# A decoder step on one Trainium2 core: cached keys and values laid out with 16 rows of one sample on each partition

## The chip, the cores and the metric

The kernel runs on one core of a Trainium2 chip. The metric is the device time of one execution in microseconds (us). A core has a matmul engine (PE, with its weight loads listed as PEld), a vector engine (DVE), an activation engine (ACT), a general engine (POOL) and a queue engine that issues most transfers (SP). Each engine works through its own queue in the order in which the program was built, and its head waits until what it needs has been signalled.

## The reference, cut to what matters

One step of a two-layer decoder is computed for a prompt group (256 positions of one sequence) and a sample group (8 samples, one position each) that share the weights. All data is fp32. Each layer has two SwiGLU blocks, a mixer and a cross attention. The change concerns the cross attention of the 8 samples, whose keys and values come from a cache in memory (256 rows, 4 heads, 256 numbers per head, for each sample and layer: 8 MB of keys and 8 MB of values per layer).

```python
def cross_attn(x, mk, mv, w_q, w_o):
    B, T, D = x.shape
    q = (x @ w_q).reshape(B, T, X_HEADS, X_HEAD_DIM)
    s = jnp.einsum('bthd,bnhd->bhtn', q, mk.astype(q.dtype)).astype(jnp.float32) / math.sqrt(X_HEAD_DIM)
    p = jax.nn.softmax(s, axis=-1).astype(x.dtype)
    o = jnp.einsum('bhtn,bnhd->bthd', p, mv.astype(x.dtype)).reshape(B, T, D)
    return o @ w_o
...
    y_sample, conv_s, rec_s = trunk(x_sample, state_conv, state_rec, cache_mem_k, cache_mem_v)
```

## The kernel before, in words

Activations lie transposed: the model dimension on the 128 partitions, the 256 prompt positions and 8 samples side by side as 264 columns. Every large product is made of three matmuls (each factor is split into a high and a low part; low times low is left out), lines 300 to 302 for the projections and 826 to 828 for the prompt's keys and values (tile `kv`). The weights come in pieces of 512 KB into the tiles `raw` (line 94, issued by SP); ACT rounds each to `wh` (line 105), and DVE or POOL subtracts to make `wl` (line 117). In the four `kv` blocks of an attention stage the subtraction is on POOL, since `W.lo` is set to `("p",)` there.

`attention(l, norm, nxt)` runs once per layer. It projects the queries of four heads (`project`, tile `qT` per head), makes the prompt's keys and values head by head (`do_kv`, 48 matmuls each, in 8 pieces of 6), and then the output projection. Smaller work is written as Python generators in three lanes; between pieces of large matmuls `flow.tick()` lets each lane emit its next piece up to the next `yield`. So a lane's piece lands on every engine's queue between two pieces of the large product. Lane 0 holds the samples: `sample_scores(h)` for four heads, then `sample_rest`. Lane 1 holds the prompt's attention: `transpose_k` (PE tile `pkt`, DVE copy to `KTt`), `prompt_scores` (PE `psc`, softmax with DVE `mxp` and ACT and DVE `Pp`, PE transposes `ppt`, then ACT `PTh` and DVE `PTl`) and `prompt_values` (PE `po`, ACT `oh`, DVE `ol`). `Vh` and `Vl` (lines 843 and 844) are the split values of the prompt. A scheduler that builds the program may move pieces within each engine's queue by data and by its own priorities; what it made is read from the built order.

The samples, before. Keys come through a ring of four 1 MB tiles (`Ring`, four free slots; a slot is refilled when `ring.done` is called). A key tile of `fill_k(h, hf)` holds one head of four samples; partition p holds rows p and 128 + p of each of them. `sample_scores(h)`:

- ACT copies the 8 query columns of head h to `zq`, rounded; DVE subtracts to put the rest 32 columns further (line 868).
- Two PE transposes (`pz`, line 872) and an ACT copy make `qn`: the queries as rows.
- For each sample a PE matmul with a picked column as weights (`pick`, line 880, tile `pb`) puts this sample's query of 256 numbers on all 128 partitions. They are issued in pairs: 4 pairs per head, 16 per layer, 32 in the program.
- For each sample and each half of its rows DVE multiplies a key row with the query and adds up (line 885, `tensor_tensor_reduce`, tile `junk`; a second short instruction writes the sum to `sc`): 16 per head, 64 per layer.

`sample_rest`: PE turns `sc` (`pst`, line 962, 2 transposes), a softmax over 32 rows of 256 follows on DVE and ACT (lines 903 to 911), PE turns it back (`psp`, line 968), DVE spreads it (line 970) into `PTs`, where the other samples' columns are zero. Then for each sample b and each half of its rows, four matmuls (one per head, line 979, tile `spv`) with a value tile of sample b (`fill_v(b)`, line 639). Each value tile gives its ring slot back after its 8 matmuls.

Of the kernel before, what the change touches and what calls it, by code (L numbers as in the profile page):

```python
# [16 lines left out]
P = 128  # L17
# [10 lines left out]
RH = 8  # L28
EPS = 1e-6
# [187 lines left out]
def trunk_step(ctx: ExitStack, tc: tile.TileContext, ins, consts, outs, stop=None):  # L217
# [22 lines left out]
    sel = cp.tile([P, NB], F32R, name="sel")  # L240
    fs, ks, vs = (cp.tile([P, RH, NB], F32, name=n) for n in ("fs", "ks", "vs"))
# [280 lines left out]
    def prepare():  # L522
# [64 lines left out]
        nc.vector.tensor_add(sel, ident[:, :NB], ident[:, 32 : 32 + NB])  # L587
        mt = ring.tiles["masks"]
# [37 lines left out]
    def add_cache(l):  # L626
        def fill_k(h, hf):
            def f(t):
                rows = ins["cache_mem_k"][l, 4 * hf : 4 * hf + 4].rearrange("b n h d -> (b n) h d")
                nc.sync.dma_start(  # L630
                    t.rearrange("p (c d) -> p c d", d=XD), rows[:, h].rearrange("(c p) d -> p c d", p=P)
                )

            return f

        def fill_v(b):
            def f(t):
                rows = ins["cache_mem_v"][l, b].rearrange("(t p) h d -> p t (h d)", p=P)
                nc.sync.dma_start(t.rearrange("p (t e) -> p t e", t=2), rows)
# [6 lines left out]
        for b in range(NB):  # L646
            ring.add((l, "v", b), fill_v(b))
# [137 lines left out]
    def attention(l, norm, nxt):  # L785
        with tc.tile_pool(name="at", bufs=1) as ap:
# [5 lines left out]
            sc = ap.tile([P, 2, XH * NB], F32, name="sc")  # L792
            PTs = ap.tile([P, 2, XH, 9 * NB], F32, name="PTs")
            os = ap.tile([P, XD], F32, name="os")
            nc.gpsimd.memset(PTs, 0.0)
            nc.gpsimd.memset(os, 0.0)
            zq = ap.tile([P, 2, P], F32, name="zq")
            nc.gpsimd.memset(zq, 0.0)
# [64 lines left out]

            def sample_scores(h):
                qT, z = qTs[h], zq
                zr = z.bitcast(F32R)
                nc.scalar.copy(zr[:, :, :NB], qT[:, :, T:])
                nc.vector.tensor_sub(z[:, :, 32:40], qT[:, :, T:], z[:, :, :NB])
                yield
                pz = aux_bank("pz")  # L870
                for dt in range(2):
                    nc.tensor.transpose(pz[:, dt * P : dt * P + P], z[:, dt], ident)
                qn = ap.tile([P, XD], F32R, tag="qn", name="qn", bufs=2)
                nc.scalar.copy(qn, pz[:, :XD])
                yield
                for b2 in range(NB // 2):
                    pb = aux_bank("pb")
                    t = ring.tiles[l, "k", h, b2 // 2].rearrange("p (b t d) -> p b t d", b=4, t=2)
                    for i in range(2):
                        nc.tensor.matmul(pb[:, i * XD : i * XD + XD], pick(2 * b2 + i), qn, start=True, stop=True)  # L880
                    for i in range(2):
                        b = 2 * b2 + i
                        for nt in range(2):
                            junk = ap.tile([P, XD], F32, tag="junk", name="junk", bufs=1)
                            nc.vector.tensor_tensor_reduce(  # L885
                                junk,
                                t[:, b % 4, nt],
                                pb[:, i * XD : i * XD + XD],
                                1.0,
                                0.0,  # L890
                                ALU.mult,
                                ALU.add,
                                sc[:, nt, h * NB + b : h * NB + b + 1],
# [596 lines left out]
```

## Time and profile before

| what | value |
|---|---|
| median of 3 runs (lowest, highest) | 1320.15 us (1319.61, 1321.84) |
| time of the profiled execution | 1320.33 us |
| its span in the trace | 1318.5 us |
| granted TensorE clock, mean | 0.996 |
| attention of layer 0, of layer 1 (about) | 300 to 395 us, 1000 to 1110 us |

Times in the trace are in us from the start of the span. A busy share of PE counts a matmul from its start to its modelled end, and matmuls overlap, so what one costs in a stream is read from the distance between starts. In a row of the timeline stand the start, the duration, engine, line, operation, output and inputs with their shapes, and in brackets the idle time just before and what ended it. In a row of windows stand the stretch, its length, then for PE, PEld, DVE, ACT and POOL the busy us and the count, then the granted clock, the share of the DMA engines and GB/s.

### The profile page before, as it was taken

Reading aid. Unit: us, or ns where it says so; the run is one execution under the profiler, and the core shown is the slowest. Engines: PE = TensorE matmul, PEld = TensorE weight load, DVE = VectorE, ACT = ScalarE, POOL = GpSimd, SP = SyncE. Lnnn points to the kernel's source line nnn. Section 1 sums busy time; section 2 is a strip of 40 time slices with the busy share of each in tenths; the row PEclk is TensorE's granted clock in tenths of the full one; section 3 lists DMA queues with packets and bytes.
Section 4 is the critical chain, followed back from the end, with each engine's and each line's share of the span. In section 5 each row is a group of like instructions: output and inputs, shape, how many; then the busy total and the mean of one; then the engine's idle time right before and its main releaser. Section 6 shows DMA issues by size and latency. Waiting matters only on the chain. (4 is left out here: it accounts for less than half of the span.)

```text
span 1318.5 us, 26128 instructions
## 1 busy us (share of the span) xinstructions
PE 1295.1 (98%) x10392; PEld 1251.1 (95%) x10392; DVE 827.2 (63%) x1570; ACT 688.2 (52%) x1121; POOL 294.1 (22%) x240
## 2 busy tenths in 40 slices
PE   8999999999999999999999999999999999999997
PEld 7999999999868999999999999999999788999996
DVE  6555567759825655556555445978699637766454
ACT  6454444455445545544555544655664446666442
POOL 3211331221732111132111231000023531211220
PEclk9999999999999999999999999999999999999998
DMA  8796555646997666656666556555457994776650
GB/s 280 224 301 180 167 183 177 192 153 204 347 362 210 195 178 178 182 169 192 188 180 178 179 176 188 161 171 162 133 159 242 386 331 131 238 208 208 193 175 34
DMA packets 265147, 266.75 MB, mean 202 GB/s; under 512 B 8697, under 2 KB 259577, under 8 KB 265026
## 3 DMA queue, kind: packets, MB, share of 16 engines
q1 hardware_dynamic: 259198, 259.78, 63.6%
q10 hardware_dynamic: 5828, 5.32, 1.2%
q8 instruction: 81, 1.33, 0.4%
q14 instruction: 40, 0.33, 0.1%
HBM read 255.00 MB, written 10.07 MB: 201 GB/s over the span
## 5 line engine op out<-in xcount | busy, mean ns | idle before, releaser
L117 DVE TENSOR_TENSOR wl<-raw,wh 128x1024 fp32r<-128x1024 f32 (+1 forms) x347 | 425.2, 1230 | 247.1 <-ACT wh L105 232.5
L300 PE MATMUL pj<-xh,wh 128*128 128x264 f32 x1952 | 560.6, 287 | 2.0 <-DVE xT L717 2.0
L301 PE MATMUL pj<-xl,wh 128*128 128x264 f32 x1952 | 553.5, 284 | 0.0
L302 PE MATMUL pj<-xh,wl 128*128 128x264 f32 x1952 | 552.8, 283 | 0.0
L105 ACT CAST wh<-raw 128x1024 fp32r<-128x1024 f32 (+1 forms) x406 | 415.1, 1032 | 256.2 <-PE pj L301 137.5
L300 PEld LDWEIGHTS pj<-xh,wh 128*128 128x128 f32 x1952 | 367.6, 188 | 4.1 <-DVE xT L717 2.9
L301 PEld LDWEIGHTS pj<-xl,wh 128*128 128x128 f32 x1952 | 368.0, 189 | 0.3
L302 PEld LDWEIGHTS pj<-xh,wl 128*128 128x128 f32 x1952 | 366.2, 188 | 0.0
L300 PE MATMUL dn<-ah,wh 128*128 128x264 f32 x704 | 200.9, 285 | 0.0
L302 PE MATMUL dn<-ah,wl 128*128 128x264 f32 x704 | 200.0, 284 | 0.0
L301 PE MATMUL dn<-al,wh 128*128 128x264 f32 x704 | 199.4, 283 | 0.0
L117 POOL TENSOR_TENSOR wl<-raw,wh 128x1024 fp32r<-128x1024 f32 (+1 forms) x61 | 143.4, 2356 | 202.9 <-ACT wh L105 135.9
L683 POOL TENSOR_TENSOR al<-a,ah 128x264 fp32r<-128x264 f32 x88 | 90.0, 1025 | 417.9 <-ACT ah L682 417.7
L302 PEld LDWEIGHTS dn<-ah,wl 128*128 128x128 f32 x704 | 132.6, 188 | 0.0
L300 PEld LDWEIGHTS dn<-ah,wh 128*128 128x128 f32 x704 | 132.4, 188 | 0.2
L301 PEld LDWEIGHTS dn<-al,wh 128*128 128x128 f32 x704 | 132.5, 188 | 0.0
L280 ACT ACTIVATE g<-g 128x264 f32<-128x264 f32 x88 | 37.0, 424 | 80.4 <-DVE g L675 80.0
L682 ACT CAST ah<-a 128x264 fp32r<-128x264 f32 x88 | 36.0, 413 | 65.1 <-DVE a L681 64.7
L322 ACT ACTIVATE xh<-xT,gains 128x264 fp32r<-128x264 f32 x56 | 28.8, 514 | 77.1 <-DVE xT L709 59.2
L885 DVE CUSTOM_DVE_ANT_0 junk<-ring,pb 128x256 f32<-128x256 f32 x128 | 53.7, 419 | 6.2
L681 DVE TENSOR_TENSOR a<-g,pj 128x264 f32<-128x264 f32 x88 | 37.1, 425 | 28.7 <-PE pj L302 28.6
L675 DVE TENSOR_TENSOR g<-pj,R_norm_ffn 128x264 f32<-128x264 f32 x88 | 37.4, 429 | 27.1 <-PE pj L302 27.0
(322 smaller groups left out, 1524.7 us busy)
## 6 DMA issues: line engine op xcount, KB each, us to landing
raw<-in_w_ffn_gate_dram SPq DMA_DIRECT2D x88, 512.0 KB, 4.9
raw<-in_w_ffn_up_dram SPq DMA_DIRECT2D x88, 512.0 KB, 3.9
raw<-in_w_ffn_down_dram SPq DMA_DIRECT2D x64, 512.0 KB, 3.5
ring<-in_cache_mem_k_dram SPq DMA_DIRECT2D x16, 1024.0 KB, 8.5
raw<-in_w_xkv_dram SPq DMA_DIRECT2D x64, 256.0 KB, 4.0
ring<-in_cache_mem_v_dram SPq DMA_DIRECT2D x16, 1024.0 KB
raw<-in_w_rec_in_dram SPq DMA_DIRECT2D x32, 512.0 KB, 4.7
raw<-in_w_ffn_down_dram SPq DMA_DIRECT2D x32, 384.0 KB, 3.0
```

The source lines that it names most:

```text
L105: self.pin(copy(wh[:, :n], self.raw[i][:, :n]))
L117: self.pin(eng.tensor_sub(wl[:, :n], self.raw.pop(i)[:, :n], wh[:, :n].bitcast(F32)))
L280: in_line(nc.scalar.activation(dst, src, func, **kw))
L300: nc.tensor.matmul(ps, wh[:, s], rh, start=first, stop=False)
L301: nc.tensor.matmul(ps, wh[:, s], rl, start=False, stop=False)
L302: nc.tensor.matmul(ps, wl[:, s], rh, start=False, stop=last)
L322: pin(nc.scalar.activation(h, src, AF.Copy, scale=g))
L675: nc.vector.tensor_mul(g, ps, norm.R)
L681: nc.vector.tensor_mul(a, g, ps)
L682: nc.scalar.copy(ah[:, blk], a)
L683: nc.gpsimd.tensor_sub(al[:, blk], a, ah[:, blk].bitcast(F32))
L885: nc.vector.tensor_tensor_reduce(junk, t[:, b % 4, nt], pb[:, i * XD : i * XD + XD], 1.0, 0.0, ALU.mult, ALU.add, sc[:, nt, h * NB + b : h ...
```

## The change

The cached rows are dealt out differently. With `NI = 16`, partition `16 b + g` now holds the 16 consecutive rows `16 g` to `16 g + 15` of sample b, for the keys as for the values. A key tile holds 8 of these 16 rows of one head for all samples; a value tile holds 2 of the 16 rows with all heads. In memory a partition's rows lie 64 KB apart (4 KB before); a piece of a key tile is still 1 KB long, a piece of a value tile is 8 KB (4 KB before). Tile sizes and their number stay as they were.

Since each partition belongs to one sample, one spread of the queries per head serves all rows: ACT copies the 8 columns, each 16 times, to `zq` (128 x 256), two PE transposes make `pq`, and all 16 DVE steps of the head read `pq`. The subtraction on DVE, the copy `qn` and the `pb` matmuls are gone.

The softmax stays on the 128 partitions: DVE takes each partition's maximum (`mxs`), PE turns it (`pst`), DVE takes the maximum over the 16 partitions of a sample (`top`) and spreads it (`tops`), PE turns it back, DVE scales it, ACT does four exponentials of 128 x 16 with sums, PE adds the sums over the 16 partitions with the matrix `peers`, DVE takes the reciprocal and makes `Ps` in four steps (a product of the exponentials, the reciprocal, and `own`, a 128 x 8 matrix that is 1 where the partition belongs to the sample). The value product has as many matmuls of the same shape as before; its weights are `Ps[:, h, i]`.

```diff
     def add_cache(l):
         def fill_k(h, hf):
             def f(t):
-                rows = ins["cache_mem_k"][l, 4 * hf : 4 * hf + 4].rearrange("b n h d -> (b n) h d")
-                nc.sync.dma_start(
-                    t.rearrange("p (c d) -> p c d", d=XD), rows[:, h].rearrange("(c p) d -> p c d", p=P)
-                )
+                rows = ins["cache_mem_k"][l].rearrange("b (g i) h d -> (b g) i h d", i=NI)
+                nc.sync.dma_start(t.rearrange("p (i d) -> p i d", d=XD), rows[:, 8 * hf : 8 * hf + 8, h])
...
-        def fill_v(b):
+        def fill_v(i2):
             def f(t):
-                rows = ins["cache_mem_v"][l, b].rearrange("(t p) h d -> p t (h d)", p=P)
-                nc.sync.dma_start(t.rearrange("p (t e) -> p t e", t=2), rows)
+                rows = ins["cache_mem_v"][l].rearrange("b (g i) h d -> (b g) i (h d)", i=NI)
+                nc.sync.dma_start(t.rearrange("p (i e) -> p i e", i=2), rows[:, 2 * i2 : 2 * i2 + 2])
...
             def sample_scores(h):
-                qT, z = qTs[h], zq
-                zr = z.bitcast(F32R)
-                nc.scalar.copy(zr[:, :, :NB], qT[:, :, T:])
-                nc.vector.tensor_sub(z[:, :, 32:40], qT[:, :, T:], z[:, :, :NB])
-                yield
-                pz = aux_bank("pz")
+                zq = ap.tile([P, 2, P], F32, tag="zq", name="zq", bufs=1)
+                nc.scalar.copy(zq.rearrange("p t (b g) -> p t b g", b=NB), spread(qTs[h][:, :, T:]))
+                yield
+                pq = aux_bank("pq")
                 for dt in range(2):
-                    nc.tensor.transpose(pz[:, dt * P : dt * P + P], z[:, dt], ident)
-                qn = ap.tile([P, XD], F32R, tag="qn", name="qn", bufs=2)
-                nc.scalar.copy(qn, pz[:, :XD])
-                yield
-                for b2 in range(NB // 2):
-                    pb = aux_bank("pb")
...
-                        nc.tensor.matmul(pb[:, i * XD : i * XD + XD], pick(2 * b2 + i), qn, start=True, stop=True)
...
+                    nc.tensor.transpose(pq[:, dt * P : dt * P + P], zq[:, dt], ident)
+                yield
+                for i in range(NI):
+                    t = ring.tiles[l, "k", h, i // 8].rearrange("p (i d) -> p i d", d=XD)
+                    junk = ap.tile([P, XD], F32, tag="junk", name="junk", bufs=1)
+                    nc.vector.tensor_tensor_reduce(
+                        junk, t[:, i % 8], pq[:, :XD], 1.0, 0.0, ALU.mult, ALU.add, sc[:, h, i : i + 1]
+                    )
+                    if i % 8 == 7:
+                        ring.done((l, "k", h, i // 8))
+                    if i % 4 == 3:
+                        yield
...
             def sample_rest():
...
+                nc.vector.reduce_max(mx, sc, axis=AX.X)
+                yield
                 pt = aux_bank("pst")
...
+                nc.tensor.transpose(pt[:XH, :P], mx, ident)
+                nc.vector.reduce_max(top, pt[:XH, :P].rearrange("h (b g) -> h b g", b=NB), axis=AX.X)
+                nc.vector.tensor_copy(tops.rearrange("h (b g) -> h b g", b=NB), spread(top))
+                yield
+                nc.tensor.matmul(pt[:, P : P + XH], tops, ident[:XH, :XH], start=True, stop=True)
+                nc.vector.tensor_scalar(mx, pt[:, P : P + XH], -1.0 / 16.0, None, op0=ALU.mult)
+                for h in range(XH):
+                    act(
+                        sc[:, h], sc[:, h], AF.Exp, bias=mx[:, h : h + 1], scale=1.0 / 16.0, accum_out=zs[:, h : h + 1]
                     )
                 yield
+                nc.tensor.matmul(pt[:, P + XH : P + 2 * XH], peers, zs, start=True, stop=True)
+                nc.vector.reciprocal(rz, pt[:, P + XH : P + 2 * XH])
+                for h in range(XH):
+                    nc.vector.scalar_tensor_tensor(
+                        Ps[:, h],
+                        sc[:, h].unsqueeze(2).broadcast_to([P, NI, NB]),
+                        rz[:, h : h + 1],
+                        own.unsqueeze(1).broadcast_to([P, NI, NB]),
+                        op0=ALU.mult,
+                        op1=ALU.mult,
+                    )
+                yield
                 ps = aux_bank("spv")
...
+                for i in range(NI):
+                    t = ring.tiles[l, "v", i // 2].rearrange("p (i h d) -> p i h d", i=2, h=XH)
+                    for h in range(XH):
+                        nc.tensor.matmul(
+                            ps[32 * h : 32 * h + NB, :XD], Ps[:, h, i], t[:, i % 2, h], start=i == 0, stop=i == NI - 1
+                        )
+                    if i % 2 == 1:
+                        ring.done((l, "v", i // 2))
+                        yield
```

The built order of PE differs between the two kernels only inside the two attention stages. On PE, in layer 1, the queue of the kernel before between the second `kv` block and the prompt values of the first head reads as follows (`pst` turns the samples' scores, `po` are the prompt values of the first head).

```order
L826 MATMUL kv_0_12655<-wh_12426,mh 128x512
L827 MATMUL kv_0_12655<-wl_12450,mh 128x512
L828 MATMUL kv_0_12655<-wh_12426,ml 128x512
L962 MATMUL pst<-ident,sc 32x128
L300 MATMUL po<-PTh,Vh_12420 128x256
L301 MATMUL po<-PTl,Vh_12420 128x256
L962 MATMUL pst<-ident,sc 32x128
L302 MATMUL po<-PTh,Vl_12421 128x256
```

On PE, at the same place of the changed kernel, the 12 `po` matmuls and 12 `kv` matmuls stand ahead of the first matmul of the softmax; its three matmuls (`pst` from `mxs`, from `tops`, from `zss`) follow over the next rows, the third among the four `psc` matmuls a few rows further.

```order
L829 MATMUL kv_1_12543<-wl_12359,mh 128x512
L830 MATMUL kv_1_12543<-wh_12338,ml 128x512
L957 MATMUL pst<-ident,mxs 4x128
L858 MATMUL pkt<-ident,Kn_12503 128x128 x4
L828 MATMUL kv_0_12542<-wh_12395,mh 128x512
L829 MATMUL kv_0_12542<-wl_12421,mh 128x512
L830 MATMUL kv_0_12542<-wh_12395,ml 128x512
L828 MATMUL kv_1_12543<-wh_12395,mh 128x512
L961 MATMUL pst<-ident,tops 128x4
L829 MATMUL kv_1_12543<-wl_12421,mh 128x512
L830 MATMUL kv_1_12543<-wh_12395,ml 128x512
```

So the samples' softmax now meets PE after `po` instead of ahead of it, with one PE row in three places instead of rows in two. Between `ppt` of the first head and the first `spv`, PE has 36 `kv` matmuls and the four `psc` in the changed kernel, 32 `kv` matmuls and no `psc` in the kernel before, where the `psc` stand behind the first eight `spv`.

On DVE, in layer 1, the kernel before has the copy `KTt` and the subtraction `Vl` behind the third score step of the third head's second key tile (ring_12199; each ISA row with `junk` is one score step, the short row behind it writes its sum).

```order
L885 ISA junk,sc<-ring_12199,pb 128x256
L885 ISA sc 128x1
L860 COPY KTt_12473<-pkt 128x512
L844 TENSOR_TENSOR Vl_12421<-Vn_12413,Vh_12420 128x512
L885 ISA junk,sc<-ring_12199,pb 128x256
```

On DVE in the changed kernel they stand at the end of that head's first key tile (ring_12080).

```order
L882 ISA junk,sc<-ring_12080,pq 128x256
L882 ISA sc 128x1
L862 COPY KTt_12379<-pkt 128x512
L882 ISA junk,sc<-ring_12080,pq 128x256
L882 ISA sc 128x1
L846 TENSOR_TENSOR Vl_12333<-Vn_12325,Vh_12332 128x512
L882 ISA junk,sc<-ring_12133,pq 128x256
```

So `KTt` is copied after 7 score steps of the third head instead of 11, and `Vl` after 8. Behind it, up to the end of `Pp`, stand 11 score steps in the changed kernel (7 in the kernel before).

More of the change, by code (lines that the diff above doesn't have):

```diff
@@ L28 @@
 RH = 8
+NI = NMEM * NB // P
 EPS = 1e-6
@@ L240, in trunk_step @@
     sel = cp.tile([P, NB], F32R, name="sel")
+    own = cp.tile([P, NB], F32, name="own")
+    peers = cp.tile([P, P], F32, name="peers")
     fs, ks, vs = (cp.tile([P, RH, NB], F32, name=n) for n in ("fs", "ks", "vs"))
@@ L587, in prepare @@
         nc.vector.tensor_add(sel, ident[:, :NB], ident[:, 32 : 32 + NB])
+        nc.vector.reduce_sum(own, ident.rearrange("p (b g) -> p b g", b=NB), axis=AX.X)
+        nc.vector.tensor_copy(
+            peers.rearrange("p (b g) -> p b g", b=NB), own.unsqueeze(2).broadcast_to([P, NB, P // NB])
+        )
         mt = ring.tiles["masks"]
@@ L645, in add_cache @@
                 ring.add((l, "k", h, hf), fill_k(h, hf))
-        for b in range(NB):
-            ring.add((l, "v", b), fill_v(b))
+        for i2 in range(NI // 2):
+            ring.add((l, "v", i2), fill_v(i2))
     def add_states(key):
```

53 lines of the change are left out of this document (8 added, 45 removed).

## The prediction

> **What bounds the kernel now.** I read the busy times first, then the busy time by stretch, then the timelines of PE and DVE inside an attention stage. The page, and four stretches of the table of windows:
>
> ```profile
> PE 1295.1 (98%) x10392; PEld 1251.1 (95%) x10392; DVE 827.2 (63%) x1570; ACT 688.2 (52%) x1121; POOL 294.1 (22%) x240
> ```
> ```profile
> 300.00:395.00 95.00, 92.87 (x637) 76.16 (x636) 67.04 (x199) 45.20 (x85) 40.27 (x21) 1.00 0.92 311
> 395.00:1000.00 605.00, 602.07 (x4993) 595.39 (x4992) 379.60 (x622) 324.14 (x500) 99.56 (x92) 1.00 0.59 177
> ...
> 1020.00:1030.00 10.00, 10.00 (x53) 8.45 (x51) 9.13 (x30) 4.38 (x10) 5.44 (x3) 1.00 1.08 376
> ...
> 1040.00:1050.00 10.00, 10.00 (x73) 6.47 (x75) 3.84 (x11) 4.28 (x10) 4.10 (x3) 1.00 1.07 392
> ```
>
> PE is busy all along, so a matmul taken off it is worth its place in the stream. But 63% of DVE is an average: while the samples' scores are made (1020 to 1030) DVE is at 91%. And the DMA engines, at 59% between the two attention stages, are at 92% in the first and above 100% in parts of the second. So two other resources stand close behind PE exactly where the change works.
>
> What a `pb` pair costs is read from the distance of starts, not from its 0.4 us:
>
> ```profile
> 1021.37 0.40 PE L880 MATMUL pb<-qn,sel 128*128 128x256 f32 x2
> 1021.60 0.60 PE L856 MATMUL pkt<-ident,Kn 128*128 128x128 f32 x4
> 1021.96 0.48 PE L826 MATMUL kv<-wh,mh 128*128 128x512 f32 x1
> 1022.28 0.40 PE L827 MATMUL kv<-wl,mh 128*128 128x512 f32 x1
> 1022.51 0.40 PE L828 MATMUL kv<-wh,ml 128*128 128x512 f32 x1
> ...
> 1031.63 0.60 PE L933 MATMUL ppt<-ident,Pp 128*128 128x128 f32 x4
> ...
> 1036.89 0.39 PE L828 MATMUL kv<-wh,ml 128*128 128x512 f32 x1
> 1038.25 0.28 PE L962 MATMUL pst<-ident,sc 128*32 128x128 f32 x1 [0.97 <-DVE sc L885]
> ...
> 1040.03 0.60 PE L856 MATMUL pkt<-ident,Kn 128*128 128x128 f32 x4
> ...
> 1043.52 1.05 PE L979 MATMUL spv<-ring,PTs 128*8 128x256 f32 x16
> 1044.50 1.99 PE L919 MATMUL psc<-KTt,qT 128*128 128x256 f32 x8
> 1046.14 0.58 PE L828 MATMUL kv<-wh,ml 128*128 128x512 f32 x1
> ...
> 1058.46 1.05 PE L979 MATMUL spv<-ring,PTs 128*8 128x256 f32 x16
> ```
> ```profile
> L880 PE MATMUL pb<-qn,sel x64: 274/279/283, 319.8 to 1033.6; 128*128 128x256 f32 x64
> ```
>
> A pair takes 0.23 to 0.24 us of the stream, the four transposes of `pkt` (or `ppt`) 0.36, a `kv` matmul 0.23 (a `po` has half its columns: 0.12), eight `spv` 0.98, four `psc` 1.6. The one place in these rows where PE stands still is `pst`: it waits for the last score step of DVE, which has fallen behind.
>
> **The change part by part.** All places are of layer 1; layer 0 has the same rows 677.2 us earlier:
>
> ```profile
> 361.01 0.29 PE L962 MATMUL pst<-ident,sc 128*32 128x128 f32 x1 [1.09 <-DVE sc L885]
> ```
>
> The sum is made against the profiled execution, 1320.33 us (span 1318.5 and 1.8 around it); the median of the runs is 0.2 below it.
>
> *The `pb` matmuls.* 64 matmuls, 32 pairs, at 0.235 us: 7.5 us, if PE doesn't wait for others instead.
>
> *The old wait at `pst`.* The `kv` matmul at 1036.89 would let the next one start at 1037.12; twelve `po` at 0.12 would be through at 1038.56, but `pkt` starts at 1040.03. With about 0.1 for `pst` itself, 1.4 us per layer are lost. In the changed order `po` comes ahead of the softmax, so this wait goes: 2.8 us in both layers. What is late next is asked below.
>
> *DVE.* Its work decides whether PE's gain stays. The score steps are as many as before, 64 per layer, with the same operands. Rows of DVE and POOL:
>
> ```profile
> 1006.90 2.11 DVE L868 TENSOR_TENSOR zq<-qT,zq 128x16 f32<-128x16 f32 x1
> ...
> 1023.33 0.68 DVE L860 COPY KTt<-pkt 128x512 f32<-128x512 f32 x1
> 1023.93 2.40 DVE L844 TENSOR_TENSOR Vl<-Vn,Vh 128x512 fp32r<-128x512 f32 x1
> ...
> 1027.17 0.42 DVE L885 CUSTOM_DVE_ANT_0 junk<-ring,pb 128x256 f32<-128x256 f32 x1
> ...
> 1027.63 0.42 DVE L885 CUSTOM_DVE_ANT_0 junk<-ring,pb 128x256 f32<-128x256 f32 x1
> ...
> 1030.48 0.17 DVE L909 RECIPROCAL zsp<-zsp 128x2 f32<-128x2 f32 x1 [0.77 <-ACT Pp L280]
> ...
> 1030.89 0.61 DVE L911 TENSOR_SCALAR Pp<-Pp,zsp 128x256 f32<-128x256 f32 x2
> ```
> ```profile
> L868 DVE TENSOR_TENSOR zq<-qT,zq x8: 167/169/2115, 317.2 to 1017.5; 128x16 f32<-128x16 f32 x8
> ```
> ```profile
> L844 DVE TENSOR_TENSOR Vl<-Vn,Vh x8: 669/692/2516, 346.6 to 1079.1; 128x512 fp32r<-128x512 f32 x8
> ```
> ```profile
> 1006.57 4.77 POOL L117 TENSOR_TENSOR wl<-raw,wh 128x1024 fp32r<-128x1024 f32 x2 [20.50 <-DMA raw<-in_w_xkv_dram]
> ...
> 1023.39 5.19 POOL L117 TENSOR_TENSOR wl<-raw,wh 128x1024 fp32r<-128x1024 f32 x2 [3.14 <-ACT wh L105]
> ```
>
> A score step follows the last one after 0.46 us, with a little more at each change of sample 0.47. The subtraction that goes is 0.17 us as a rule, but the third took 2.11: it began just after POOL's first `wl` and ended when that one did (half of 4.77 behind 1006.57 is 1008.96). `Vl` took 2.40 in the same way, against about 0.69 undisturbed. The score steps, one operand of which is in PSUM, are not slowed while POOL works: the two above lie within POOL's 5.19 from 1023.39. So DVE gains 2.1 + 0.1 us ahead of `KTt`. The built order has `KTt` four score steps earlier (1.9 us): 1023.33 - 2.2 - 1.9 = 1019.2. The transposes `pkt` under it end near 1019.2 as well (1021.60 less 12 pairs, 2.8, plus 0.4). `KTt` (0.6 from start to start) and a score step bring `Vl` to about 1020.5. POOL's pair of `wl` hangs on the `kv` evacuation by ACT, which has 9 pairs ahead of it: 1023.39 - 2.1 = 1021.3. So `Vl` (0.6) is through 0.2 us ahead of POOL. Behind it stand 11 score steps (5.2), and `mxp`, its scaling, the reciprocal and `Pp`. These four took 1.1 before: from the end of `Vl`, 1026.33, to that of `Pp`, 1031.50, less 7 score steps and 0.77 idle; I take 1.3. `Pp` ends at 1027.6. PE wants it for `ppt` at 1031.63 - 15 pairs, 1028.1. It doesn't wait, by 0.5 us.
>
> *The new softmax on PE.* From `ppt` at 1028.1, PE has 0.36 + 12 `kv` + 12 `po` + 12 `kv` (2.8, 1.4, 2.8): it reaches `pst` at 1035.4. DVE has five score steps, `PTl`, eight score steps, `Vl` (both 128 x 512, 0.6 each) and the maximum (0.2) behind 1027.6: 1035.1. Then three round trips, bounded by these rows:
>
> ```profile
> L970 DVE COPY PTs<-psp x4: 195/198/200, 365.3 to 1042.7; 128x32 f32<-128x32 f32 x4
> ```
> ```profile
> L1331 DVE SCALAR_TENSOR_TENSOR ring<-pb,ks,ring x64: 335/342/353, 1116.0 to 1221.5; 128x128 f32<-128x128 f32 x64
> ```
> ```profile
> 994.30 0.20 ACT L867 CAST zq<-qT 128x16 fp32r<-128x16 f32 x1
> ...
> 995.88 0.37 ACT L874 CAST qn<-pz 128x256 fp32r<-128x256 f32 x1 [0.43 <-PE pz L872]
> ...
> 1029.43 0.47 ACT L280 ACTIVATE Pp<-psc,mxp 128x256 f32<-128x256 f32 x1 [3.81 <-DVE mxp L904]
> ...
> 1029.89 0.47 ACT L280 ACTIVATE Pp<-psc,mxp 128x256 f32<-128x256 f32 x1
> ```
>
> (1) `pst` 0.3, `top` 0.2, `ol` 0.6 (it stands between), `tops` 0.2: 1.3 to 1.5 us, against 0.1 + 0.36 + 4 x 0.23 = 1.4 of PE work. (2) Behind `tops`, `KTt` 0.6 covers the matmul; then a scaling 0.2 and four exponentials with sums, each 0.46 as in the rows above at most, and 0.29 if 16 columns instead of 256 save here what they save between the two casts (0.17). With 0.1 for the handovers 2.1 to 2.7 us, against 3 `kv` and 3 `psc` (0.7 + 1.2 = 1.9). (3) `peers` 0.3, reciprocal 0.15, four steps at 0.25 to 0.34: 1.5 to 1.8, against `psc` and 5 `kv` (1.6). So the waits are 0.2 to 1.1 us per layer; I take 0.7, near the middle, since no row pulls it to one end. In both layers 1.4.
>
> *The rest.* ACT's spread copy has the size of the `qn` cast that goes. Two `psp` and two `pst` transposes go for three small matmuls: 0 to 0.3 us per layer, taken as 0.1, in both layers 0.2. `own` and `peers` are made on DVE ahead of the first transposes, while these wait for the first transfers; without that cover two steps of 0.2 us. POOL loses two memsets that nobody waits for. The value products are the same matmuls (0.98 us for eight).
>
> *Transfers.* As many bytes, queued on SP in almost the same order. Here the layout could cost; the rows:
>
> ```profile
> ring<-in_cache_mem_k_dram SPq DMA_DIRECT2D x16, 1024.0 KB, 8.5
> ```
> ```profile
> 1048.46 2.93 SPq L639 DMA_DIRECT2D ring<-in_cache_mem_v_dram  x2
> ```
>
> The median key tile lands 8.5 us after its issue; for a value tile I take the same. The first of these two is the sixth value tile, read at 1058.46: 10.0 us after issue, 1.5 to spare. In the changed order 29 `kv`, 12 `po`, `ppt`, `pkt` and three blocks of `spv` lie between the step that frees that slot and the one that reads it, 11.8 us: 3.3 to spare. If pieces of 1 KB at 64 KB steps move as those at 4 KB did, nothing waits: cost 0. No row shows otherwise, in either direction: faster transfers would gain nothing, since PE doesn't wait for them now.
>
> Sum: 7.5 + 2.8 - 1.4 - 0.1 (small matmuls and the start, between -0.2 and +0.4) = 8.8 us. 1320.33 - 8.8 = 1311.5 us.
>
> **The rivals.**
>
> *DVE falls behind at `ppt`* (0.20). If `Vl` comes 0.2 to 0.8 us later, POOL's `wl` holds it: 2.40 instead of 0.69. `Pp` then ends at 1029.5 to 1030.2 and PE waits 1.4 to 2.1 us at `ppt`; the later steps start from there, and 0.3 of the next wait goes. Both layers: about 3.5 us back, 1315.0 us. For it: that is what happened to `Vl` in both layers before. Against: the new place in the order. [...]
>
> *The gain is eaten by waits of the new chain* (0.12). If the maximum, `tops` or `Ps` are held by POOL, each by up to one `wl` (2.4 us), two of three in a layer cost 4.4 us net of the cover: both layers 8.8, 1320.3 us, no change. It decides from 3 us per layer on. Against: POOL is busy 5.4 of 10 us at 1020 and 4.1 at 1040, so two hits in both layers are rare.
>
> *The transfers get slower* (0.08). Twelve ring tiles (four of keys, eight of values) are issued within the full stretch of a layer; at 392 GB/s they take 32.1 us. If the new steps cost a third of the rate, they take 48, and less the 3.3 to spare PE waits 12.7 us per layer: 1311.5 + 25.4 = 1336.9 us, slower. It decides from a rate a fifth lower, where 4.4 us per layer are lost and the gain is gone. For it: the DMA share is above 1.0. Against: the pieces aren't smaller, and the weights, read at other steps, reach the same rate. The Trainium skill, DMA: Bandwidth & Descriptors, section Latency and other measured facts, speaks against the layout: rows per partition that lie a large power of two apart ran at 207 GB/s for 512 KiB, 164 for 2 MiB and 103 for 4 MiB, against 214 in full, and it calls the cause an inference. No run here shows it; 64 KB is below its list, and its figure for 512 KiB would be 3%, within the spare time.
>
> **How the numbers follow.** The forecast has 0.60, its own range 1308.5 to 1313.0: without any wait it is 1.4 less, and if the rest of PE's idle time goes too (95.00 - 92.87 - 1.09 = 1.0 per stage) 2.0 less; the dear ends give 0.8 and 0.4 more, rounded up. With the first rival and the lower edge of the second the range is 1308.5 to 1318.0; some 0.16 is left out. About 0.2% (2.6 us) is what a measurement can tell from no change. Below 1317.5: forecast and first rival, 0.80. Within: the second, 0.12. Above: the third, 0.08.
>
> **What would show it.** Right: no `pb` rows; PE goes from the last `kv` ahead of `po` without a gap; each attention stage about 4.4 us shorter, everything else equal; waits at the three `pst` matmuls and the first `spv` below 1.5 us together. First rival: a `Vl` of over 2 us in each layer, and PE idle at `ppt` behind `Pp`. Second: `top`, `tops` or `Ps` at over 2 us, PE idle before `spv`. Third: DVE idle on a key tile or PE on a value tile, and a lower GB/s in both stages. The forecast is wrong if the stages shrink by less than 3 us or more than 6 us each.

## The result and the profile after

| | before | after |
|---|---|---|
| median of 5 runs each, us | 1320.15 | 1311.04 |
| lowest to highest, us | 1319.41 to 1321.84 | 1310.76 to 1312.63 |
| ratio, with its 95% interval | | 0.9934 (0.9923 to 0.9944) |
| span of the profiled execution, us | 1318.5 | 1310.5 |

The kernel is 9.1 us, 0.7%, faster. The profiled execution of after is the longest of its five (1312.63 us), so the two profiles differ by 8.0 us and the medians by 9.1.

First the page's line of busy times, and the two attention stages in the table of windows:

```profile
PE 1288.9 (98%) x10330; PEld 1244.2 (95%) x10330; DVE 822.4 (63%) x1570; ACT 689.4 (53%) x1125; POOL 292.3 (22%) x236
```
```profile
300.00:390.00 90.00, 88.77 (x604) 72.62 (x607) 64.68 (x198) 44.92 (x83) 39.91 (x20) 1.00 0.93 321
995.00:1100.00 105.00, 103.08 (x698) 84.87 (x697) 64.58 (x193) 51.72 (x99) 44.72 (x22) 1.00 0.93 311
```

PE has 6.2 us less to do and DVE 4.8, no row of `pb` is left, and PE is still what is busy all along. Then two rows from the answers on two tiles, for the queries (their first start opens the stage) and for the output projection that ends it:

```profile
L814 DVE TENSOR_TENSOR qT<-pj,R_norm_xattn x16: 423/432/434, 316.4 to 1002.4; 128x264 f32<-128x264 f32 x16
L303 PE MATMUL pj<-oh,wh x128: 278/283/473, 397.0 to 1099.6; 128*128 128x264 f32 x128
```
```profile
L812 DVE TENSOR_TENSOR qT<-pj,R_norm_xattn x16: 419/432/433, 315.8 to 1008.9; 128x264 f32<-128x264 f32 x16
L300 PE MATMUL pj<-oh,wh x128: 278/283/473, 400.9 to 1107.8; 128*128 128x264 f32 x128
```

(The second pair is of before.) From the first queries to the first output projection layer 0 takes 80.6 us instead of 85.1. To see what those 4.5 us are made of, I took all of PE's matmuls in the timeline of that stage, from the first `ps_ms` to the first `pj<-oh`, and added up for each tile the distance from a start to the next start. In such a sum a wait counts on the matmul ahead of it:

| PE, layer 0, us | before | after | |
|---|---|---|---|
| `pb` | 3.76 | 0 | -3.76 |
| `kv` | 47.80 | 47.44 | -0.36 |
| `po` | 4.74 | 4.30 | -0.44 |
| `psc` | 4.92 | 4.71 | -0.21 |
| `pst` and `psp` | 0.32 | 0.56 | +0.24 |
| all others (`pj`, `spv`, `pkt`, `ppt`, `pz` or `pq`, `spt`, `ps_ms`) | 30.48 | 30.50 | +0.02 |
| sum | 92.02 | 87.51 | -4.51 |

Layer 1 has 91.80 and 87.41, 4.39 less, with the same parts to within 0.15. Together that is 8.9 us: 7.5 of it `pb`, and 1.4 the balance of waits, of the softmax's matmuls and of what stands next to what (the three `po` beside the two `pst` of before take 0.20 to 0.22 each instead of 0.12). The spans differ by 8.0: the other 0.9 us lie outside the two stages, 0.65 of them ahead of the first, whose start lies between 307.9 and 310.0 us in the profiles of the runs below.

The places on which the prediction rested, from the timelines of DVE and POOL (after, layer 1):

```profile
1015.39 0.69 DVE L862 COPY KTt<-pkt 128x512 f32<-128x512 f32 x1 [0.54 <-PE pkt L858]
...
1016.33 0.69 DVE L846 TENSOR_TENSOR Vl<-Vn,Vh 128x512 fp32r<-128x512 f32 x1
...
1032.53 0.68 DVE L959 COPY tops<-top 4x128 f32<-4x128 f32 x1
```
```profile
1016.79 4.82 POOL L118 TENSOR_TENSOR wl<-raw,wh 128x1024 fp32r<-128x1024 f32 x2 [2.40 <-PE kv L830]
...
1030.61 4.84 POOL L118 TENSOR_TENSOR wl<-raw,wh 128x1024 fp32r<-128x1024 f32 x2 [2.05 <-ACT wh L106]
```

DVE now reaches `KTt` before its transposes are there (0.54 idle), and `Vl` begins 0.46 us ahead of POOL's `wl` and takes 0.69, not 2.40. And PE around the softmax:

```profile
1024.04 0.60 PE L924 MATMUL ppt<-ident,Pp 128*128 128x128 f32 x4
...
1031.42 0.27 PE L957 MATMUL pst<-ident,mxs 128*4 128x128 f32 x1
...
1032.67 0.40 PE L828 MATMUL kv<-wh,mh 128*128 128x512 f32 x1
1033.26 0.38 PE L961 MATMUL pst<-ident,tops 4*128 4x4 f32 x2 [0.20 <-DVE tops L959]
...
1035.67 0.28 PE L968 MATMUL pst<-zss,peers 128*128 128x4 f32 x2
...
1037.25 0.40 PE L830 MATMUL kv<-wh,ml 128*128 128x512 f32 x1
1037.58 1.05 PE L984 MATMUL spv<-ring,Ps 128*8 128x256 f32 x16
```

The first `pst` waits for nothing. The second follows a `kv` after 0.59 instead of 0.23, so PE loses 0.36 us there: it waits for `tops`, a copy of 4 x 128 that took 0.68 us and ended when the first of POOL's two `wl` had (half of 4.84 behind 1030.61 is 1033.03). The third `pst` and the first `spv` wait for nothing: the `kv` ahead of this `spv` takes 0.33, as one does wherever it stands ahead of a block of `spv`, in both kernels.

### The profile page after: what moved, and what is told of

Same layout as the page of the kernel before. It is cut to its first block, busy times and chain, and to the rows that moved or that the text cites. A ratio compares the mean times of both kernels' runs of the same rounds, so it can differ in the third digit from the quotient of the medians.

```text
span 1310.5 us, 25974 instructions
## 1 busy us (share of the span) xinstructions
PE 1288.9 (98%) x10330; PEld 1244.2 (95%) x10330; DVE 822.4 (63%) x1570; ACT 689.4 (53%) x1125; POOL 292.3 (22%) x236
## 4 chain that ended last, share of the span: by engine, by line
PE 92%; DVE 4%; ACT 2%; issue 1%; DMA 1%; POOL 0%; DVEq 0%; SPq 0%; ACTq 0%; POOLq 0%
PE pj L303 19%; PE pj L304 19%; PE pj L305 19%; PE dn L303 7%; PE dn L305 7%; PE dn L304 6%; PE kv L828 2%; PE kv L830 2%; PE kv L829 2%; DVE wl L118 1%; PE spv L984 1%; DVE xl L327 1%; PE psc L910 1%; PE pl L1139 1%; PE pj L370 1%; ACT wh L106 1%
## 5 line engine op out<-in xcount | busy, mean ns | idle before, releaser
L882 DVE CUSTOM_DVE_ANT_0 junk<-ring,pq 128x256 f32<-128x256 f32 x128 | 53.6, 419 | 3.7
```

What stands on the lines that cost most here:

```text
L882: nc.vector.tensor_tensor_reduce(junk, t[:, i % 8], pq[:, :XD], 1.0, 0.0, ALU.mult, ALU.add, sc[:, h, i : i + 1])
```

## The experiments

The theory: the gain is the stream time of the `pb` matmuls, plus the old wait, less the new ones; and it comes out as time only because DVE keeps ahead of POOL's `wl` at a few places. Rivals: the transfers' new layout gained something; DVE's lighter work or the softmax's new place alone gained it.

**e2_old_loads.** The changed kernel with the transfers of before.

```diff
-rows = ins["cache_mem_v"][l].rearrange("b (g i) h d -> (b g) i (h d)", i=NI)
-nc.sync.dma_start(t.rearrange("p (i e) -> p i e", i=2), rows[:, 2 * i2 : 2 * i2 + 2])
+rows = ins["cache_mem_v"][l, i2].rearrange("(t p) h d -> p t (h d)", p=P)
+nc.sync.dma_start(t.rearrange("p (t e) -> p t e", t=2), rows)
```

(and the keys in the same way; with the new layout the rows of neighbouring partitions lie 64 KB apart in memory, with this one 4 KB)

> The changed kernel with the transfers of the kernel before: keys and values come into the same tiles by the old address patterns, so rows of other samples are scored and summed. Every instruction of the engines stays. If the layout of the transfers costs or gains nothing, as the prediction took it, 1311 us (1310 to 1312). If part of the gain came from the new patterns, 1313 us or more; if they cost something, 1309 us or less.

Measured: 1310.96 us, ratio to before 0.9932 (0.9919 to 0.9945), where the changed kernel has 0.9934. The layout neither gains nor costs time here. The windows show the same rate, 317 and 310 GB/s against 321 and 311, and the median key tile lands 8.4 us after its issue, against 8.5:

```profile
300.00:390.00 90.00, 88.61 (x600) 71.92 (x599) 63.43 (x196) 44.96 (x84) 40.76 (x20) 1.00 0.94 317
995.00:1100.00 105.00, 103.09 (x697) 84.86 (x697) 63.82 (x189) 52.09 (x100) 45.63 (x24) 1.00 0.94 310
```

**e1c_pb_end.** The changed kernel with idle `pb` matmuls at a place where nobody notices them.

```diff
 nc.scalar.copy(os[32 * h : 32 * h + NB], ps[32 * h : 32 * h + NB, :XD])
 yield
+pb = aux_bank("pb")
+for b in range(32):
+    nc.tensor.matmul(pb[:, b % 2 * XD : b % 2 * XD + XD], pick(b % 8), mh[:, 0], start=True, stop=True)
+yield
```

> The changed kernel with as many idle spread matmuls as the kernel before had (32 of 128x256 per layer, 64 in all), but in one row behind the last value products of each layer, into a bank nobody reads. No other instruction changes its place on DVE or ACT, and nobody waits for them. My theory: they cost their place in PE's stream and nothing else, 64 x 0.117 = 7.5 us: 1311.0 + 7.5 = 1318.5 us (1318 to 1319). If PE's time was not what the change saved, they disappear in PE's waits and it stays near 1311 us.

Measured: 1319.31 us (1317.52 to 1319.97), ratio 0.9989 (0.9980 to 0.9997): 8.3 us above the changed kernel, where 7.5 was expected; the interval of the ratio allows both. In PE's timeline the row of 32 takes 3.74 us from its start to the next one's, 7.5 in both layers:

```profile
390.30 3.91 PE L995 MATMUL pb<-mh,sel 128*128 128x256 f32 x32
394.04 0.40 PE L828 MATMUL kv<-wh,mh 128*128 128x512 f32 x1
```

That settles the largest term: a `pb` matmul costs 0.117 us of PE's stream, though its row says 0.28, and that stream is what the kernel's time follows.

**e1_pb_back.** The same matmuls, but where they used to stand. Here score steps wait for them (12.0 us of DVE in 18 places), which in the kernel before none did for its `pb`.

```diff
 for i in range(NI):
+    if i % 4 == 0:
+        for b in range(i // 2, i // 2 + 2):
+            nc.tensor.matmul(pq[:, XD:], pick(b), mh[:, 0], start=True, stop=True)
     t = ring.tiles[l, "k", h, i // 8].rearrange("p (i d) -> p i d", d=XD)
```

> The changed kernel with the 64 spread matmuls put back as idle ones: two of 128x256 ahead of every four score steps, with the old stationary selector and the first 256 columns of mh as the moving operand, into the unused half of the pq bank, which nobody reads. The score steps and the softmax stay new. If what the change gained is PE's stream (32 pairs at 0.235 us), 7.5 us of it go: 1311.0 + 7.5 = 1318.5 us (1317.5 to 1319.5). If it came from DVE's lighter work, from the softmax's new place or from the transfers, PE takes the pairs into its idle time and the kernel stays at 1311 to 1313 us.

Measured: 1325.22 us, ratio 1.0046 (1.0032 to 1.0060). Both theories missed it, mine by 6.7 us. The profiled execution is the longest of the five, 1329.29 us (three lie at 1325.1 to 1325.2), so it shows the places and not the exact price. PE's sum by tiles has 4.0 us more per layer for the pairs, as expected. Another 1.0 per layer goes to the first `spv` block, taken apart as in e5 below, and in layer 0 PE has half its granted clock for 3.4 us (368.6 to 372.0). The rest lies in waits that the changed kernel doesn't have (rows of PE's waits, then of DVE and POOL in layer 0):

```profile
PE pst L964 <- DVE tops L962: 3.4, 2, 1.7
...
PE spv L987 <- DVE Ps L974: 1.3, 2, 0.7
```
```profile
365.34 2.01 DVE L962 COPY tops<-top 4x128 f32<-4x128 f32 x1
...
372.99 3.27 DVE L974 SCALAR_TENSOR_TENSOR Ps<-sc,rzs,own 128x128 f32<-128x128 f32 x4
```
```profile
362.56 4.71 POOL L118 TENSOR_TENSOR wl<-raw,wh 128x1024 fp32r<-128x1024 f32 x2 [3.79 <-DMA raw<-in_w_xkv_dram]
373.76 2.36 POOL L118 TENSOR_TENSOR wl<-raw,wh 128x1024 fp32r<-128x1024 f32 x1 [6.49 <-ACT wh L106]
```

`tops` took 2.01 us and ended with POOL's pair at 367.27; `Ps` took 3.27 instead of 1.14, with a `wl` in the middle of it. The new softmax chain has the same steps as in the changed kernel; its place has moved, against POOL and in the built order (the first `pst` stands seven `kv` later). This is the second rival of the prediction, in a kernel where it came true.

**e3_one_pb** and **e34_both.** The other way round: PE's saving alone, on the kernel before.

```diff
-for b2 in range(NB // 2):
-    pb = aux_bank("pb")
+pb = aux_bank("pb")
+for i in range(2):
+    nc.tensor.matmul(pb[:, i * XD : i * XD + XD], pick(i), qn, start=True, stop=True)
+for b2 in range(NB // 2):
     t = ring.tiles[l, "k", h, b2 // 2].rearrange("p (b t d) -> p b t d", b=4, t=2)
-    for i in range(2):
-        nc.tensor.matmul(pb[:, i * XD : i * XD + XD], pick(2 * b2 + i), qn, start=True, stop=True)
```

> The kernel before with one pair of spread matmuls per head instead of four: all score steps of a head read the queries of the first two samples, so three quarters of the scores are other ones. The old softmax keeps its old place. It takes 24 pairs from PE, 5.6 us at 0.235. If only PE's stream counts, 1320.1 - 5.6 = 1314.5 us. My theory: DVE's score steps, 0.46 us each, are not fewer, DVE has little idle time ahead of the softmax, and PE then waits at pst for what it has saved ahead of it, 2.8 us per layer less what DVE's idle time gives up; so 1317 to 1320 us, with a wait at pst of 2.5 to 3.8 us per layer instead of 1.0.

e34_both adds the edit of e4_late_softmax, below.

> Both edits on the kernel before: one pair of spread matmuls per head, and the old softmax one step later. It has neither the new layout of keys and values nor the softmax in place. My theory: 5.6 + 2.8 = 8.4 us less if both terms are independent, 1311.7 us; if DVE is what PE then waits for at pst, about 2 us per layer of that stay behind: 1315 us. If the change's gain needs the new layout or the softmax in place, 1317 us or more.

Measured: 1332.79 us, ratio 1.0094 (1.0079 to 1.0110), and 1330.57 us, ratio 1.0080 (1.0068 to 1.0093). With 5.6 us less work on PE the kernels are 12 and 10 us slower. Neither theory had that. In e3, layer 0, from DVE's, POOL's and PE's timelines:

```profile
329.18 2.12 DVE L868 TENSOR_TENSOR zq<-qT,zq 128x16 f32<-128x16 f32 x1 [0.17 <-ACT zq L867]
...
344.96 2.40 DVE L844 TENSOR_TENSOR Vl<-Vn,Vh 128x512 fp32r<-128x512 f32 x1
...
351.33 1.32 DVE L904 TENSOR_SCALAR mxp<-mxp 128x2 f32<-128x2 f32 x1
...
354.75 2.72 DVE L911 TENSOR_SCALAR Pp<-Pp,zsp 128x256 f32<-128x256 f32 x2
```
```profile
344.43 5.20 POOL L117 TENSOR_TENSOR wl<-raw,wh 128x1024 fp32r<-128x1024 f32 x2 [2.70 <-ACT wh L105]
350.25 2.38 POOL L117 TENSOR_TENSOR wl<-raw,wh 128x1024 fp32r<-128x1024 f32 x1 [0.62 <-DMA raw<-in_w_xkv_dram]
354.72 2.34 POOL L117 TENSOR_TENSOR wl<-raw,wh 128x1024 fp32r<-128x1024 f32 x1 [2.09 <-ACT wh L105]
```
```profile
357.36 0.45 PE L933 MATMUL ppt<-ident,Pp 128*128 128x128 f32 x1 [5.13 <-DVE Pp L911]
```

The subtraction (beside a `wl` from 328.86 to 331.27), `Vl`, the scaling of `mxp` and the first of the two `Pp` each began just behind the start of a `wl` and ended with it, `Vl` half a us later. PE, early by its saved matmuls, stands 5.1 us at `ppt` in each layer and 1.5 to 1.7 at `psp`. The long wait has a second price, seen in the windows behind it (the column after the engines is the granted clock):

```profile
357.00:358.00 1.00, 0.64 (x2) 0.52 (x3) 0.96 (x5) 0.00 (x0) 0.06 (x1) 0.64 1.03 410
358.00:360.00 2.00, 2.00 (x8) 1.68 (x7) 1.18 (x5) 0.58 (x1) 0.00 (x0) 0.50 1.22 347
360.00:362.00 2.00, 2.00 (x9) 1.65 (x8) 1.86 (x10) 0.58 (x2) 0.00 (x0) 0.83 0.79 267
```

PE comes back at half its clock and has it in full 3.3 us after its first matmul; in layer 1 it takes 6.0 us. The Trainium skill, TensorE: Matmul & The Clock Gate, section Part 1: The HAM clock gate, says that after about 3.4 us without work PE runs at half rate until it has been busy for as long; layer 0 agrees, and in layer 1 half rate lasts longer. Half rate also follows shorter waits here, which that rule does not cover: from 370.9 to 374.3 in this layer 0, 0.6 us behind a wait of 1.65 us at `psp`, and in e1 1.2 us behind one of 1.75. Waits of 1.5 to 2.0 us in e4 and e6 have no such stretch behind them, and why is open.

**e8_one_pb_no_sub.** e3 without the eight subtractions of the queries' low part.

```diff
-nc.vector.tensor_sub(z[:, :, 32:40], qT[:, :, T:], z[:, :, :NB])
```

> The kernel of e3 (the kernel before with one spread pair per head, so three quarters of the scores read other queries) without the subtraction that makes the low part of the queries (zq on DVE, L868), so the spread carries the rounded queries alone. Eight instructions go from DVE, 0.17 us each but for two of 2.12; PE's, ACT's and POOL's order stay as in e3. My theory: in e3 each of zq, Vl, the scaling of mxp and Pp began behind a wl of POOL and was held; without zq's 2.0 us per layer Vl starts near 342.9 us, ahead of the wl at 344.4, the later holds go with it, and the 24 pairs come out as time: 1320.4 - 5.6 - 2.5 (the wait at pst) = 1312 us, up to 1316 if one hold per layer stays. If DVE's load as such is what e3 ran into (64 score steps of 0.46 us), only the subtractions' own time comes back: 1332.8 - 4.2 = 1328.6 us.

Measured: 1318.61 us (1317.04 to 1320.68), ratio 0.9988 (0.9979 to 0.9997). Eight instructions that took 5.2 us of DVE in e3 are worth 14.2 us. `Vl` starts at 343.40, ahead of POOL, and takes 0.69. It is still 6.6 us above my 1312, and the waits say where most of it is: 2.4 us per layer are at places where `Pp` and, behind the second `Vl`, `Ps` came late.

```profile
PE psp L967 <- DVE Ps L910: 3.4, 2, 1.7
...
PE ppt L932 <- DVE Pp L910: 1.4, 2, 0.7
```
```profile
361.03 2.62 DVE L844 TENSOR_TENSOR Vl<-Vn,Vh 128x512 fp32r<-128x512 f32 x1
```

**e7_no_sub.** The same edit on the kernel before, with all its `pb`.

> The kernel before without the subtraction for the low part of the queries (zq on DVE; the spread carries the rounded queries alone); all spread matmuls and the order of PE, ACT and POOL stay. DVE is 2.0 us per layer earlier from the third head on. My theory: KTt then waits for pkt, Vl starts 0.5 us ahead of POOL's wl instead of behind it, DVE is some 3.5 us ahead at the last score step, and PE's wait at pst (1.25 us per layer) goes, but no more, since PE's stream is as long as before: 1320.2 - 2.5 = 1317.7 us. If DVE's holds set the time of the kernel before throughout, 1313 us; if they cost nothing there, 1320 us.

Measured: 1319.30 us, ratio 0.9994 (0.9985 to 1.0003), which can't be told from no change. In its profile the mechanism is there:

```profile
344.83 0.68 DVE L844 TENSOR_TENSOR Vl<-Vn,Vh 128x512 fp32r<-128x512 f32 x1
```
```profile
344.88 5.25 POOL L117 TENSOR_TENSOR wl<-raw,wh 128x1024 fp32r<-128x1024 f32 x2 [2.90 <-ACT wh L105]
```

`Vl` slips in 0.05 us ahead of POOL, PE waits for no score step, and the stage of layer 0 is 0.8 us shorter (91.23 by the sum). Ahead of `pst` 1.07 us are gone, but 0.28 came back at `psp`. So DVE being earlier was worth 0.8 us per layer on that kernel, not my 1.25, and DVE's lighter work alone is not what the change gained.

**e4_late_softmax.** The old softmax one step later, nothing else.

```diff
 nh = XH * NB
+yield
 pt = aux_bank("pst")
```

> The kernel before with the old softmax one step later (one more yield ahead of pst), so that po stands ahead of it as in the changed kernel; all 64 spread matmuls stay. My theory: the wait at pst goes, 1.4 us per layer, and nothing comes in its place: 1320.1 - 2.8 = 1317.3 us. If the new place of the softmax is what the change gained, 1311 to 1313 us. If the old wait only turns up at psp or at the first spv, 1319 to 1320 us.

Measured: 1322.29 us, ratio 1.0017 (1.0008 to 1.0026): slower by 2. The wait at `pst` is gone, and another stands at `psp`, since the scaling of `Ps` now falls into a `wl`:

```profile
PE psp L969 <- DVE Ps L911: 3.0, 2, 1.5
```
```profile
365.70 1.91 DVE L911 TENSOR_SCALAR Ps<-Ps,zss 32x256 f32<-32x256 f32 x1
```
```profile
365.11 2.36 POOL L117 TENSOR_TENSOR wl<-raw,wh 128x1024 fp32r<-128x1024 f32 x1 [0.51 <-DMA raw<-in_w_xo_dram]
```

A later place alone gains nothing, at least for the old softmax.

**e6_vl_late.** The first rival, made to happen: 0.6 us ahead of the first `Vl`.

```diff
+if h == 0:
+    dm = ap.tile([P, 2], F32, name="dm")
+    nc.vector.reduce_max(dm, vh.bitcast(F32), axis=AX.X)
 nc.vector.tensor_sub(vl, vn, vh.bitcast(F32))
```

> The changed kernel with one more DVE instruction ahead of the first Vl of each layer: a maximum over Vh into a tile nobody reads, 0.6 us, one SBUF input, not held by POOL. Vl then starts near 1016.9 us instead of 1016.3, and POOL's wl at 1016.8. My theory (the first rival of the prediction, made to happen): Vl is held to the end of that wl, 2.4 us instead of 0.69, Pp comes 2.3 us later, PE waits some 2 us at ppt in each layer: 1311.0 + 4 = 1315 us (1313.5 to 1317). If DVE has the slack that its busy share of 63% suggests, 1311 us.

Measured: 1320.83 us (1318.69 to 1323.90), ratio 1.0006 (0.9997 to 1.0015): two instructions of 0.6 us, and the whole gain is gone. `Vl` was held as foreseen, but most of the price fell elsewhere: PE waits 0.9 us at `ppt` in layer 0 and 0.15 in layer 1, and 2.0 at `tops` in each.

```profile
342.82 2.77 DVE L849 TENSOR_TENSOR Vl<-Vn,Vh 128x512 fp32r<-128x512 f32 x1
...
360.45 2.27 DVE L962 COPY tops<-top 4x128 f32<-4x128 f32 x1
```
```profile
PE pst L964 <- DVE tops L962: 4.0, 2, 2.0
```

The built order moved too (`ol` stands ahead of the maximum now, `pst` six `kv` later), and the first block of value products is taken apart between `kv` matmuls. So the edit isn't the late `Vl` alone, and I don't split its 9.8 us further; the profiled execution, 1318.69 us, is the shortest of its runs.

**e5_tops_act.** The copy `tops` on ACT.

```diff
-nc.vector.tensor_copy(tops.rearrange("h (b g) -> h b g", b=NB), spread(top))
+nc.scalar.copy(tops.rearrange("h (b g) -> h b g", b=NB), spread(top))
```

> The changed kernel with the copy of the maxima (tops) on ACT instead of DVE. In the changed kernel this 4x128 copy took 0.67 us twice and ended when POOL's first wl had ended, where the 128x128 copy of peers took 0.23. My theory: it was held, ACT takes 0.2 to 0.3 us, and the 0.36 us that PE stands at the second pst go in each layer: 1311.0 - 0.7 = 1310.3 us. If the copy is just that long, or the wait is for ACT's own queue, 1311 us or more.

Measured: 1314.62 us, ratio 0.9957 (0.9944 to 0.9970): slower than the changed kernel by 3.6. The copy takes 0.29 us and PE no longer waits for it, as the theory had it. But the builder took the first `spv` block apart, 2 + 1 + 5 between `kv` matmuls (e5, layer 0, PE; a row counts each of these products twice, a block of eight is x16):

```profile
364.07 0.66 PE L984 MATMUL spv<-ring,Ps 128*8 128x256 f32 x4
364.66 0.50 PE L828 MATMUL kv<-wh,mh 128*128 128x512 f32 x1
365.09 0.60 PE L984 MATMUL spv<-ring,Ps 128*8 128x256 f32 x2
365.62 0.50 PE L829 MATMUL kv<-wl,mh 128*128 128x512 f32 x1
366.05 1.03 PE L984 MATMUL spv<-ring,Ps 128*8 128x256 f32 x10
```

The one that stands alone takes 0.53 us from start to start, where one in a whole block takes 0.12, and each `kv` behind such a piece 0.43 instead of 0.23. By the sum over the layer `spv` takes 8.95 instead of 7.84. That is 2.2 us for both layers, most of the loss; the rest I haven't traced.

**f1_act_yield** and **f4_tops_psum_yield.** Both keep the `spv` blocks whole by one more `yield` ahead of them. f1 has the copy on ACT; f4 leaves it on DVE as another operation, with an operand in PSUM:

```diff
-nc.vector.tensor_copy(tops.rearrange("h (b g) -> h b g", b=NB), spread(top))
+nc.vector.scalar_tensor_tensor(
+    tops.rearrange("h (b g) -> h b g", b=NB), spread(top), 1.0,
+    pt[:XH, :P].rearrange("h (b g) -> h b g", b=NB), op0=ALU.mult, op1=ALU.max
+)
```

> The changed kernel with the copy of the maxima on ACT as in e5, and one more yield ahead of the value products, so that their first block isn't taken apart between kv matmuls as it was in e5 (where spv took 8.95 us per layer of PE's stream instead of 7.85). My theory: the 0.36 us at the second pst go, the spv stay at 7.85 and no wait is left in the chain: 1311.0 - 0.7 = 1310.3 us (1309.5 to 1310.8). If the later start of the value products makes value tiles late, 1312 us or more.

> The changed kernel with the copy of the maxima made by DVE as a scalar_tensor_tensor step, the maximum of the spread top (SBUF) and the transposed maxima (PSUM), which gives the same numbers, and one more yield ahead of the value products. It has as many SBUF inputs as the copy, but it isn't a copy. My theory: the copy was held by POOL's wl and this step isn't, as the score steps with an operand in PSUM aren't: 0.2 to 0.3 us instead of 0.67, and 1310.3 us as in f1. If the 0.67 us were due to something else (4 partitions, the steps of zero), it takes 0.67 us again and PE waits at pst as before: 1311 us.

Measured: 1311.27 us, ratio 0.9938 (0.9925 to 0.9950), and 1311.43 us, ratio 0.9936 (0.9924 to 0.9949). In f4 the step took 0.26 us in the middle of a `wl` of POOL's:

```profile
359.03 0.26 DVE L959 SCALAR_TENSOR_TENSOR tops<-top,pst 4x128 f32<-4x128 f32 x1
```
```profile
357.08 4.85 POOL L118 TENSOR_TENSOR wl<-raw,wh 128x1024 fp32r<-128x1024 f32 x2 [2.03 <-ACT wh L106]
```

So the copy's 0.67 us were a hold by POOL. The wait for `tops` is gone in both, but the time is that of the changed kernel. Up to the last matmul of the output projection PE's sums are 0.2 us shorter per layer and not 0.36, and either is less than the runs of one kernel scatter (1310.65 to 1313.03). No version here beats the changed one by a measurable amount.

## Why the prediction was right

The forecast was 1311.5 us and the median is 1311.04.

- *The `pb` matmuls, 7.5 us.* Shown: 3.76 us per layer in before's stream, 3.74 in e1c's, 8.3 us by e1c's median.
- *The old wait, 2.8 us, and the new ones, 1.4, with the small matmuls 0.1.* Their balance, 1.3 us, was right: the sum over PE without `pb` falls by 0.75 in layer 0 and 0.63 in layer 1. The old wait was read well: 1.25 and 1.13 us of standing still ahead of `pst`, and 0.25 in the `po` beside it. That the other parts add up is partly luck. The new waits are 0.36 per layer, at `tops` alone, half of the 0.7 taken; the softmax's small matmuls are 0.24 per layer dearer, and other changes of neighbours take 0.15, where 0.1 was taken for both layers. Nor is the old wait to be had by itself: e7 gained 0.8 us per layer and e4 nothing, since it came back at `psp`. In the changed kernel PE has other matmuls to do during each step of the chain, and only `tops` outlasted them.
- *DVE.* The order came out as forecast: `KTt` comes together with its transposes (it waits 0.54), `Vl` slips ahead of POOL (0.46 us, forecast 0.2), `Pp` is in time for `ppt`, though by 0.15 and not 0.5. This was the step on which everything hung. e3, e8 and e6 show what stands on it: PE's saving with `Vl` held is a loss of 12 us, and with it free a gain of 1.6.
- *The round trips.* The first took 1.84 us from `pst` to `tops`' matmul where 1.3 to 1.5 was forecast: `tops`, taken as 0.2, was 0.67. This step was mis-sized, and by a mechanism I had: I had taken an instruction with one SBUF input to be safe from POOL. The kernel before already shows otherwise: the two `Pp` at 372.46 took 1.72 us beside a `wl` that began at 371.38, against 0.61 for the pair at 1030.89. The Trainium skill, SBUF — State Buffer, section Who interferes with whom, calls an instruction with one SBUF input safe only outside the two-port modes, which copies and `tensor_scalar` can enter, and the runs agree: `tops` up to 2.27 us, the scaling of `mxp` 1.32, `Ps` 1.91, against 0.14 to 0.34 undisturbed. The second trip was through in 1.9 us, at the end of the exponentials (forecast 2.1 to 2.7; they follow one another by 0.29, the cheap end), and the third in 1.75 (1.5 to 1.8), with `Ps` not held. PE's own matmuls filled 2.4 and 1.9 us there, more than the 1.9 and 1.6 taken as cover, so it waited at neither.
- *Transfers, 0.* Shown by e2. The third rival falls with it.
- *The rivals.* The first and the second are real mechanisms that the changed kernel missed by fractions of a us, the second not wholly (`tops`): e6 is the first, e1 the second, and e4 shows the same hold in the old chain. My price for the first, 1315.0, looks too low: in e6 the late `Vl` pushed the softmax into the next `wl`, and it came to 1320.8, though its built order had moved too.

## What to carry to other kernels

Work taken off the engine that bounds a kernel is worth its place in the stream (the distance of starts, not the length of its rows), but only while the engines that feed it keep ahead; look first for what they would run into when everything comes earlier. Write down for each DVE (VectorE) step of a short chain whether POOL (GpSimd) can hold it (two SBUF inputs, or a copy or scaling from SBUF to SBUF) and how far it starts from POOL's next instruction: here 0.6 us more on DVE per layer, with the shift in the built order that it brought, took back 9.8 (e6). And an experiment that puts one part back shifts all the others in time, so read its profile before its time is taken for the price of that part.

## What the runs showed of the hardware

- A copy of 4 x 128 words on DVE takes 0.67 to 2.27 us when POOL is at work, and one of 128 x 128 (`peers`, at the kernel's start) 0.23; the same result with an operand in PSUM takes 0.26 under the same `wl` (f4).
- After 5.1 us without work PE ran at a granted clock of 0.50, and in full again 3.3 us after its first matmul in layer 0 and 6.0 in layer 1 (e3): a long wait costs more than its length. Waits of 1.65 and 1.75 us were each followed by 3.4 us at 0.50 (e3, e1), those of 2.0 us in e6 were not.
- Eight value products in one row take 0.98 us of PE; cut into 2 + 1 + 5 by `kv` matmuls they made the layer's `spv` 1.1 us dearer (e5; in e6 1.0).
- Keys and values whose rows lie 64 KB apart from partition to partition in DRAM came as fast as those at 4 KB: all transfers of layer 0's stage together 321 and 317 GB/s, the median key tile 8.5 and 8.4 us from issue to landing (after and e2).
